# One matmul for folded squares, a first gate pair in the common order, and a smaller first transfer

## The chip, the cores and the metric

The kernel runs on one core of one Trainium2 chip. The metric is the device time of one execution in microseconds (us). Engines are named as in the profile: PE is the matrix engine (PEld its weight loads), DVE the vector engine, ACT the scalar engine, POOL the general-purpose engine, SP the one that issues most transfers. A name with q (SPq, ACTq) is an engine's issue of a transfer.

## The reference

One layer over 512 tokens of width 2048, in float32. Three token mixers run side by side on projections of the same normalised input; C is stick-breaking attention, B chunked attention with a relative bias, A attention with forget gates. Each has four heads of width 128.

```python
hn = rmsnorm(x, norm_g)
proj = jnp.einsum('bsd,dc->bsc', hn, w_in)
br = proj[..., :QKVG_COLS].reshape(b, s, N_BRANCH, 4, BRANCH_W)   # q, k, v, g of A, B, C
gates = jax.nn.sigmoid(proj[..., QKVG_COLS + N_HEADS:] + b_gate).reshape(b, s, N_BRANCH, D_MODEL)
qa = rmsnorm(to_heads(br[:, :, 0, 0]), qk_norm_g[0])              # likewise ka, qb, kb; not in C
...
ys = jnp.stack([from_heads(ya), from_heads(yb), from_heads(yc)], axis=2) * jax.nn.silu(br[:, :, :, 3])
up = jnp.einsum('bsnw,nwd->bsnd', ys, w_up)
merged = jnp.sum(gates * up, axis=2)
return x + jnp.einsum('bsd,de->bse', merged, w_out)
```

## The kernel before

Everything is held transposed: a tile has 128 features on the partitions and the 512 tokens along the row. To keep float32 accuracy each operand is split into a high part in the matrix engine's reduced format and a low part, the rest (`split`: ACT copies the high part, DVE subtracts for the low one). A product is then high x high, high x low and low x high.

The projections come as pairs of 128-column blocks (`PairTask`). A pair is computed by Strassen's scheme on the two halves of the tokens (256 each) and the two halves of the 2048 inputs, with seven products, numbered 1 to 7. Each product is a unit (`Pair`) of eight steps over the inputs. In the usual form a step of the high weight part reads both parts of x at once as one matmul of 512 columns, and a step of the low weight part reads the high x as one of 256. Products that are added up share an accumulator bank: 6 goes onto 1, 7 onto 6, 4 onto 7, 3 onto 5 (`onto`), after ACT has copied what was there. The order of these products is 1, 2, 6, 5, 7, 3, 4.

The first gate pair, which follows the first four projections, has a form of its own, chosen by `late=True`: the order 1, 5, 2, 3, 6, 7, 4, each step of the high weight part as two matmuls of 256 columns, and no sharing of banks, so that sums are done by DVE from separate banks.

A weight for a product is loaded by SP as a raw tile. Two of the five raw tiles of a pair get a second block added in the transfer (`add_up`, issued by POOL); two more sums are made by DVE (`sums`): block 1 plus block 5 is the weight of product 6, and that plus block 2 the weight of product 3. `prep` splits a weight two units ahead of its use.

The first unit group (`first_quad`) computes Q, K, V and G of head C0 as x arrives; x is also scaled by the norm's gain (`prep_x`), squared for its norm, and its Strassen combinations (t23, t4) are made in `combos`. The forget gates' logits come from small matmuls against w2 (`logits`). Sixteen matmuls on constants (WARM) run on PE before any data is there.

Q and K of the eight heads of B and A are normalised in `normed`: square the tile, split the square, multiply both parts by a matrix of ones to sum over the 128 partitions, take the reciprocal root, scale, and split again (qkh, qkl). Scores read these parts.

The order of PE, ACT and DVE is fixed in the program. A planner (`Flow`) sets it: each task yields its steps with an engine and an estimated cost, and the planner repeatedly takes the step that can start first, ties by due time. `at(u, ...)` starts a side task when unit u begins. Buffers (`Slots`) are counted there as well, so a step's place also depends on when buffers come free. What the planner doesn't order (transfers) is issued in the order in which the tasks ask.

Of the kernel before, what the change touches and what calls it, by code (L numbers as in the profile page):

```python
# [8 lines left out]
F32 = mybir.dt.float32  # L9
F32R = mybir.dt.float32r  # L10
BF16 = mybir.dt.bfloat16
AF = mybir.ActivationFunctionType
ALU = mybir.AluOpType
AX = mybir.AxisListType

P = 128
S = 512
D = 2048
HD = 128
NH = 4  # L20
W = 512
NB = 3
KT = D // P
QB = S // P
DT = D // P
UK = 8
NQ = 4
HS = S // 2
EPS = 1e-6
NEG = -1e30  # L30
SCALE = HD ** -0.5
# [4 lines left out]
PE, ACT, DVE = 0, 1, 2  # L36
# [26 lines left out]
class Flow:  # L63
# [98 lines left out]
def hybrid_kernel(  # L162
# [2 lines left out]
    xT: bass.AP,  # L165
    xn: bass.AP,
    begin: bass.AP,
    w_one: bass.AP,
    w_two: bass.AP,
    w_col: bass.AP,  # L170
# [5 lines left out]
    nc = tc.nc  # L176
    PS = bass.MemoryType.PSUM

    cp = ctx.enter_context(tc.tile_pool(name="cp", bufs=1))
# [35 lines left out]
    def blk(i):  # L215
        return slice(i * P, (i + 1) * P)
# [22 lines left out]
    def pair_of(name, dt=F32R):  # L239
        return t2(name + "h", dt), t2(name + "l", dt)  # L240

    def split(hi, lo, src, n, ev=None, due=(), hi_ev=None):

        yield (ACT, act_us(n), *due)
        nc.scalar.activation(hi, src, AF.Copy)  # L245
        if hi_ev is not None:
            set_(hi_ev)
        yield (DVE, dve_us(n), *due)
        nc.vector.tensor_sub(lo, src, f(hi))  # L249
        if ev is not None:  # L250
            set_(ev)
# [38 lines left out]

    nc.scalar.preload_act_table_set("natural_log_exp_and_others")
    begin_in = cp.tile([P, begin.shape[1]], F32, name="begin_in")
    x_begin, small_in = begin_in[:, :S], begin_in[:, S:]
    first = [tc.keep_in_program_order(nc.sync.dma_start(begin_in, begin))]
    gn = small_in[:, 0:KT]
    gqk = small_in[:, KT:KT + 4]
    bfc = small_in[:, KT + 4:KT + 5]
    bg = small_in[:, KT + 5:KT + 5 + NB * DT]
    wf = small_in[:, KT + 5 + NB * DT:].rearrange("p (k h) -> p k h", h=NH)

    epsc = cp.tile([P, 1], F32, name="epsc")
    nc.gpsimd.memset(epsc, EPS)
    nhepsc = cp.tile([P, 1], F32, name="nhepsc")
    nc.gpsimd.memset(nhepsc, -0.5 * EPS)
    tmpc = t2("tmpc")
    onef, zerof, nu_f = tmpc[:, blk(0)], tmpc[:, blk(1)], tmpc[:, blk(2)]
    nc.gpsimd.memset(onef, 1.0)
    nc.gpsimd.memset(zerof, 0.0)
    ones_r = cp.tile([P, P], F32R, name="ones_r")
    nc.vector.tensor_copy(ones_r, onef)  # L310
# [14 lines left out]
    nc.gpsimd.memset(zeroc, 0.0)  # L325

    gq = cp.tile([P, 4], F32, name="gq")
    nc.vector.tensor_copy(gq, gqk)
    for c in (0, 2):
        nc.vector.tensor_scalar_mul(gq[:, c:c + 1], gqk[:, c:c + 1], SCALE)  # L330

    w2 = cp.tile([P, KT * NH + 32], F32, name="w2")
    nc.vector.tensor_copy(w2[:, :KT * NH].rearrange("p (k h) -> p k h", k=KT), wf)
    nc.vector.tensor_copy(w2[:, KT * NH:], zerof[:, :32])
    t2s.free.pop()


# [88 lines left out]
    def prep_x(kt):  # L426

        due = (2.5 + 2.7 * place[kt],)
        yield x_in[kt]
        x, g, h, lo = xraw[kt], gn[:, kt:kt + 1], xs[kt].hi, xs[kt].lo  # L430
        if kt == 0:
            yield (DVE, 0.5, *due)
            nc.vector.tensor_scalar_mul(h, two(x), g)
        else:
            yield (ACT, act_us(S), *due)
            nc.scalar.activation(h, two(x), AF.Copy, scale=g)
        set_(raw_hi[kt])
        yield (DVE, dve_us(S), *due)
        nc.vector.scalar_tensor_tensor(lo, two(x), g, f(h), op0=ALU.mult, op1=ALU.subtract)
        set_(raw_ev[kt])  # L440

        due = (DUE[0] - 16.0 + place[kt],)
        if kt % 2 == 0:
            yield (DVE, 0.5, *due)
            nc.vector.tensor_scalar_mul(x, x, g)
# [435 lines left out]
    class Head:  # L881
# [23 lines left out]
        def normed(self, r):  # L905
            yield self.event(r)
            c = self.c[r]
            yield from by_norm(c)
            yield t2s, 3
            yield ACT, act_us(S)  # L910
            sq = t2("sq")
            nc.scalar.activation(sq, c, AF.Square)
            hi, lo = pair_of("sq")
            yield from split(hi, lo, sq, S)
            give(t2s)
            yield atts, 1
            yield PE, mm_us(S, 2)
            ps = att()
            nc.tensor.matmul(ps, ones_r, hi, start=True, stop=False)  # L919
            nc.tensor.matmul(ps, ones_r, lo, start=False, stop=True)  # L920
            give(t2s, 2)
            yield t2s, 4
            rs = t2("rs")
            yield from rsqrt(rs, ps, HD, (t2("rt"), t2("rw"), t2("rv")), S, lambda: give(atts))
            give(t2s, 3)
            i = 2 * self.n + r
            yield DVE, dve_us(S)
            nc.vector.scalar_tensor_tensor(rs, rs, gq[:, i:i + 1], c, op0=ALU.mult, op1=ALU.mult)
            give(t2s)
            yield t2s, 2  # L930
            self.c[r] = pair_of("qk")
            yield from split(*self.c[r], rs, S, self.event("p", r))
            give(t2s)
# [338 lines left out]
    def first_head(n, h):  # L1272
        hd = Head(n, h)
        units.extend(first_quad(hd))
        at(OFF["fb"], forget_bias)
        gate_units(late=True)
        schedule(hd, OFF["a0"], OFF["b0"])

    def head(n, h, last=False):
# [220 lines left out]
    def loads():  # L1500
        def x(kt):
            if kt == 0:
                xraw[kt], x_in[kt].t = x_begin, landing(0.0, 256)
                return
            yield t2s, 1
            xraw[kt] = t2("x")
            x_in[kt].t = fetch(xraw[kt], xT[kt], 0.0, 256).t

        def n(i):
            yield t2s, 1  # L1510
            t = t2("xn")
            n_in[i].t = fetch(t, xn[i // NQ, i % NQ], 0.0, 256).t
            spawn(square_x(i, t), 10.0)

        todo = list(range(NQ * QB))
        for i, sp in enumerate(spans):

            for kt in [kt for sp in spans[i:i + (2 if i > 2 else 1)] for kt in range(*sp)]:
                if xraw[kt] is None:
                    yield from x(kt)  # L1520
            yield from load_unit(units[i])
            if i >= N_FROM:
                for _ in range(N_PER):
                    if todo:
                        yield from n(todo.pop(0))
        for i in todo:
            yield from n(i)
        for u in units[len(spans):]:
            yield from load_unit(u)
# [27 lines left out]
    spawn(loads(), 0.0, 0.0)  # L1557
    for kt in range(KT):
        spawn(prep_x(kt), 5.0)
    for k in range(UK):  # L1560
        spawn(combos(k), 5.0)
    spawn(stream(), 1e9)
# [4 lines left out]
NT = 20  # L1567
KEPT = 1
AHEAD = 0.4
WARM = 16  # L1570
SPANS = [(0, 1), (1, 2)] + [(k + h, k + h + 2) for k in range(0, UK, 2) for h in (0, UK)][1:]
N_ONE = 2
NX = 28
# [56 lines left out]
```

## Time and profile before

| | |
|---|---|
| median of 3 runs | 1318.89 us (1318.42 to 1319.12) |
| profiled execution | 1318.54 us, span 1316.8 us |
| granted PE clock | 1.000 |
| PE busy | 1311.3 us (100%), 7474 matmuls |
| DVE / ACT / POOL busy | 1140.6 / 807.2 / 95.0 us |
| bytes moved | 266.24 MB, 202 GB/s |

The span is the time from the first to the last instruction in the profile; what lies around it makes up the difference to the execution's time. In rows of the timeline the columns are start, duration, engine, line, operation, what is written from what, shapes, and how many instructions were merged into the row; a bracket gives the idle time before it and what ended it. A row with several instructions has as its duration the time from the first start to the last end, and ends of matmuls are modelled, so a matmul's price is read from one start to the next.

### The profile page before, as it was taken

How to read it: one execution, taken by the hardware profiler on the slowest of the kernel's cores; microseconds unless marked ns; L12 is line 12 of the kernel's file. 1: busy time of each engine (PE TensorE's matmuls, PEld its weight loads, DVE VectorE, ACT ScalarE, POOL GpSimd, SP SyncE). 2: the span in 40 equal slices, each digit the busy share in tenths (PEclk: the TensorE clock that was granted, in tenths of full speed). 3: DMA queues.
4: the chain of work that ended last, by engine and by line, in shares of the span. 5: the costliest groups of instructions: out<-in, count | busy, mean ns of one | idle time of the engine just before them, and what ended most of it. 6: DMA issues, size and time to landing. Idle time of an engine off the chain costs nothing.

```text
span 1316.8 us, 20264 instructions
## 1 busy us (share of the span) xinstructions
PE 1311.3 (100%) x7474; PEld 1149.1 (87%) x7474; DVE 1140.6 (87%) x1707; ACT 807.2 (61%) x1280; POOL 95.0 (7%) x120
## 2 busy tenths in 40 slices
PE   9999999999999999999999999999999999999998
PEld 6898888888888888888888888888888888898887
DVE  8999989788898889888898989889899988897786
ACT  8766757575557665666656664666657655454443
POOL 0010100000010100101000000001000000000100
PEclk9999999999999999999999999999999999999999
DMA  9777767767776776766767767776769765668883
GB/s 339 213 204 198 183 192 185 200 186 192 201 199 187 188 200 179 219 181 189 202 179 216 188 184 199 205 185 185 195 179 280 248 219 168 206 172 253 242 248 100
DMA packets 89651, 266.24 MB, mean 202 GB/s; under 512 B 10560, under 2 KB 12608, under 8 KB 89552
## 3 DMA queue, kind: packets, MB, share of 16 engines
q1 hardware_dynamic: 70400, 203.86, 45.5%
q0 software_dynamic: 15552, 56.63, 25.4%
q10 hardware_dynamic: 3600, 4.46, 0.9%
q8 instruction: 59, 0.97, 0.3%
q14 instruction: 40, 0.33, 0.1%
HBM read 245.21 MB, written 19.70 MB: 201 GB/s over the span
## 4 chain that ended last, share of the span: by engine, by line
PE 99%; DVE 1%; DMA 0%; ACT 0%; issue 0%; ACTq 0%
PE acc L264 85%; PE att L264 8%; PE att L1022 1%; PE att L260 1%; PE att L1136 1%; PE att L261 1%; PE att L1137 1%; PE att L259 1%; PE att L1135 1%; PE att L1087 0%; PE att L1237 0%; PE att L919 0%; PE att L920 0%; DMA begin_in<-in_begin 0%; DVE m L249 0%; DVE wl L249 0%
## 5 line engine op out<-in xcount | busy, mean ns | idle before, releaser
L249 DVE TENSOR_TENSOR wl<-raw,wh 128x1024 fp32r<-128x1024 f32 (+2 forms) x418 | 499.0, 1198 | 122.2 <-ACT wh L245 121.5
L245 ACT ACTIVATE wh<-raw 128x1024 fp32r<-128x1024 f32 (+2 forms) x418 | 433.7, 1039 | 162.9 <-PE acc L264 89.9
L264 PE MATMUL acc<-x,wh 128*128 128x512 f32 (+1 forms) x1568 | 396.7, 388 | 0.7 <-DVE gq L330 0.7
L264 PEld LDWEIGHTS acc<-x,wh 128*128 128x128 f32 x1568 | 283.7, 188 | 56.1 <-issue 2.2
L264 PE MATMUL acc<-t,wh 128*128 128x512 f32 (+1 forms) x1128 | 280.3, 388 | 0.0
L264 PEld LDWEIGHTS acc<-t,wh 128*128 128x128 f32 x1128 | 200.4, 189 | 34.8
L264 PEld LDWEIGHTS acc<-x,wl 128*128 128x128 f32 x1504 | 205.9, 190 | 16.5 <-issue 0.8
L264 PE MATMUL acc<-x,wl 128*128 128x256 f32 (+1 forms) x1504 | 216.5, 285 | 0.0
L264 PE MATMUL acc<-t,wl 128*128 128x256 f32 x1104 | 156.5, 283 | 0.0
L264 PEld LDWEIGHTS acc<-t,wl 128*128 128x128 f32 x1104 | 144.7, 191 | 2.1
L282 POOL DMA_DIRECT2D raw<-in_w_col x92 | 79.7, 866 | 916.3 <-DMA raw<-in_w_col 449.3
L264 PE MATMUL acc<-m,wh 128*128 128x512 f32 (+1 forms) x512 | 109.7, 364 | 0.3 <-DVE m L249 0.3
L264 PEld LDWEIGHTS acc<-m,wh 128*128 128x128 f32 x512 | 86.3, 189 | 13.9 <-DVE m L249 0.5
L825 ACT ACTIVATE c<-acc 128x256 f32<-128x256 f32 x51 | 19.6, 384 | 90.8 <-PE acc L264 85.3
L771 ACT ACTIVATE u<-acc 128x512 f32<-128x512 f32 x52 | 31.1, 598 | 65.6 <-PE acc L264 60.3
L631 DVE TENSOR_TENSOR raw<-raw,raw 128x1024 f32<-128x1024 f32 x54 | 65.8, 1219 | 0.3
L637 DVE TENSOR_TENSOR raw<-raw,raw 128x1024 f32<-128x1024 f32 x54 | 65.8, 1218 | 0.3
L264 PE MATMUL att<-y,wh 128*128 128x512 f32 x256 | 65.8, 389 | 0.0
L792 ACT ACTIVATE u<-acc 128x512 f32<-128x512 f32 x51 | 30.3, 595 | 55.1 <-PE acc L264 54.2
L264 PEld LDWEIGHTS acc<-m,wl 128*128 128x128 f32 x448 | 58.3, 191 | 2.4
L264 PE MATMUL acc<-m,wl 128*128 128x256 f32 x448 | 59.8, 283 | 0.0
L264 PEld LDWEIGHTS att<-y,wh 128*128 128x128 f32 x256 | 48.0, 188 | 10.0
(202 smaller groups left out, 1388.6 us busy)
## 6 DMA issues: line engine op xcount, KB each, us to landing
raw<-in_w_col SPq DMA_DIRECT2D x230, 512.0 KB, 4.4
raw<-in_w_col POOLq DMA_DIRECT2D x92, 512.0 KB, 6.4
raw<-in_w_out SPq DMA_DIRECT2D x40, 512.0 KB, 4.3
gl<-c SPq DMA_DIRECT2D x48, 256.0 KB, 3.1
raw<-in_w_up SPq DMA_DIRECT2D x32, 384.0 KB, 3.1
sg<-gl SPq DMA_DIRECT2D x48, 256.0 KB, 4.4
raw<-in_w_out POOLq DMA_DIRECT2D x16, 512.0 KB, 7.3
xn<-in_xn SPq DMA_DIRECT2D x16, 256.0 KB, 3.6
```

Source lines behind the costliest of these rows:

```text
L245: nc.scalar.activation(hi, src, AF.Copy)
L249: nc.vector.tensor_sub(lo, src, f(hi))
L259: nc.tensor.matmul(ps, lh, rh, start=start, stop=False, skip_group_check=more)
L260: nc.tensor.matmul(ps, lh, rl, start=False, stop=False, skip_group_check=more)
L261: nc.tensor.matmul(ps, ll, rh, start=False, stop=stop, skip_group_check=more)
L264: nc.tensor.matmul(ps, w, x, start=start, stop=stop, skip_group_check=more)
L282: nc.gpsimd.dma_start(to, src, accum_op=ALU.add)
L631: nc.vector.tensor_add(w[1], w[1], w[5])
L637: nc.vector.tensor_add(w[2], w[2], w[1])
L771: nc.scalar.activation(self.u, ps, AF.Copy)
L792: nc.scalar.activation(self.s, ps, AF.Copy)
L825: nc.scalar.activation(c, ps[:, RH], AF.Copy, scale=-1.0)
```

## The change

Four things change.

1. `normed`: the lower and the upper 64 partitions of the tile are squared into two tiles of 64 partitions, and DVE adds them. The sum is split with its high part in partitions 0 to 63 and its low part in 64 to 127 of one tile, so that one matmul with the ones sums both.
2. The first gate pair loses `late=True`: product order 1, 2, 6, 5, 7, 3, 4, sums in the banks, 512-column matmuls in the high parts.
3. The first transfer (begin) holds only x's first tile and the norm gains, 528 columns instead of 645. The other constants (117 columns) are a transfer of their own, issued by ACT after its weight load. What reads them on DVE (gq, w2) becomes a planned task, `small_parts`.
4. The constant ones are written first on POOL, and WARM goes from 16 to 19.

```diff
-    x_begin, small_in = begin_in[:, :S], begin_in[:, S:]
+    small_in = cp.tile([P, consts.shape[1]], F32, name="small_in")
+    x_begin, gn = begin_in[:, :S], begin_in[:, S:]
...
+    def small_parts():
+        yield DVE, 0.8
+        nc.vector.tensor_copy(w2[:, :KT * NH].rearrange("p (k h) -> p k h", k=KT), wf)
+        nc.vector.tensor_copy(gq, gqk)
+        for c in (0, 2):
+            nc.vector.tensor_scalar_mul(gq[:, c:c + 1], gqk[:, c:c + 1], SCALE)
...
-            yield ACT, act_us(S)
-            sq = t2("sq")
-            nc.scalar.activation(sq, c, AF.Square)
-            hi, lo = pair_of("sq")
-            yield from split(hi, lo, sq, S)
+            yield ACT, act_us(S, 2)
+            sa, sb = t2("sa"), t2("sb")
+            nc.scalar.activation(sa[:HP], c[:HP], AF.Square)
+            nc.scalar.activation(sb[:HP], c[HP:], AF.Square)
+            yield DVE, dve_us(S)
+            nc.vector.tensor_add(sa[:HP], sa[:HP], sb[:HP])
+            give(t2s)
+            parts = t2("sq", F32R)
+            yield from split(parts[:HP], parts[HP:], sa[:HP], S)
             give(t2s)
             yield atts, 1
-            yield PE, mm_us(S, 2)
+            yield PE, mm_us(S)
             ps = att()
-            nc.tensor.matmul(ps, ones_r, hi, start=True, stop=False)
-            nc.tensor.matmul(ps, ones_r, lo, start=False, stop=True)
-            give(t2s, 2)
+            nc.tensor.matmul(ps, ones_r, parts, start=True, stop=True)
+            give(t2s)
...
-        gate_units(late=True)
+        gate_units()
...
+            if i == 0:
+                nc.scalar.dma_start(small_in, consts)
...
+    spawn(small_parts(), 2.0, 9.0)
...
-WARM = 16
+WARM = 19
```

The order of instructions moves at three places. DVE at the first data, before (x_113 is the high part of x's first tile and then its low part, wl_194 or wl_195 the low part of the first weight):

```order
L334 COPY w_108<-tmpc_85 128x32
L328 COPY gq<-begin_in 128x4
L333 COPY w_108<-begin_in 128x64
L433 TENSOR_SCALAR x_2_113<-begin_in 128x2x256
L330 TENSOR_SCALAR gq<-begin_in 128x1 x2
L439 TENSOR_SCALAR x_2_113<-begin_in,x_2_113 128x2x256
L445 TENSOR_SCALAR begin_in<-begin_in 128x512
L392 TENSOR_TENSOR wl_195<-raw_150,wh_194 128x512
```

and in the change:

```order
L331 COPY w_106<-tmpc_82 128x32
L438 TENSOR_SCALAR x_2_110<-begin_in 128x2x256
L444 TENSOR_SCALAR x_2_110<-begin_in,x_2_110 128x2x256
L450 TENSOR_SCALAR begin_in<-begin_in 128x512
L397 TENSOR_TENSOR wl_196<-raw_150,wh_195 128x512
```

The copies and products for gq and w2 are gone from in front of x's parts; they come back between the parts of x's third and fourth tiles.

DVE where the first gate pair is fed, before (wl_623 is the low weight part of product 5, wl_557 of 1, raw_512 plus raw_509 the weight of product 6, c_686 and c_688 are copies of the first four projections):

```order
L249 TENSOR_TENSOR wl_623<-raw_509,wh_622 128x1024
L249 TENSOR_TENSOR wl_557<-raw_512,wh_556 128x1024
L249 TENSOR_TENSOR t_92_541<-x_174,t_92_541 128x256
L1223 COPY c_686<-acc_204 128x512
L1223 COPY c_688<-att_206 128x512
L631 TENSOR_TENSOR raw_512<-raw_512,raw_509 128x1024
```

and in the change (wl_562 is the low part of product 1, wl_628 of 2, wl_695 of 6; L636 and L642 are the two sums of raw weights):

```order
L251 TENSOR_TENSOR wl_562<-raw_517,wh_561 128x1024
L251 TENSOR_TENSOR t_92_546<-x_175,t_92_546 128x256
L636 TENSOR_TENSOR raw_517<-raw_517,raw_514 128x1024
L1231 COPY c_691<-acc_205 128x512
L1231 COPY c_693<-att_207 128x512
L251 TENSOR_TENSOR wl_628<-raw_519,wh_627 128x1024
L251 TENSOR_TENSOR t_103_650<-x_181,t_103_650 128x256
L251 TENSOR_TENSOR t_101_635<-x_191,t_101_635 128x256
L251 TENSOR_TENSOR t_102_647<-x_193,t_102_647 128x256
L642 TENSOR_TENSOR raw_519<-raw_519,raw_517 128x1024
L251 TENSOR_TENSOR wl_695<-raw_517,wh_694 128x1024
```

The low part of 5 has left the front of this stretch, and the first sum has moved ahead of the two copies.

DVE at the first normalised head, K and Q of B0, before (sql are the low parts of the squares, the wl rows those of weights):

```order
L249 TENSOR_TENSOR sql_3835<-sq_3832,sqh_3834 128x512
L249 TENSOR_TENSOR wl_3851<-raw_3687,wh_3850 128x1024
L249 TENSOR_TENSOR sql_3847<-sq_3844,sqh_3846 128x512
L249 TENSOR_TENSOR wl_3887<-raw_3651,wh_3886 128x1024
L249 TENSOR_TENSOR wl_3923<-raw_3710,wh_3922 128x1024
```

and in the change (sa is a folded square of 64 partitions, sq the tile with both parts):

```order
L920 TENSOR_TENSOR sa_3799<-sa_3799,sb_3800 64x512
L251 TENSOR_TENSOR wl_3795<-raw_3635,wh_3794 128x1024
L251 TENSOR_TENSOR sq_3816<-sa_3780,sq_3816 64x512
L251 TENSOR_TENSOR sq_3820<-sa_3799,sq_3820 64x512
L251 TENSOR_TENSOR wl_3826<-raw_3599,wh_3825 128x1024
```

The two additions (the row ahead of this piece is the other) stand before the same weight part, and both low parts of the squares follow it.

More of the change, by code (lines that the diff above doesn't have):

```diff
@@ L16 @@
 P = 128
+HP = P // 2
 S = 512
@@ L167, in hybrid_kernel @@
     begin: bass.AP,
+    consts: bass.AP,
     w_one: bass.AP,
@@ L292, in hybrid_kernel @@
     begin_in = cp.tile([P, begin.shape[1]], F32, name="begin_in")
-    x_begin, small_in = begin_in[:, :S], begin_in[:, S:]
+    small_in = cp.tile([P, consts.shape[1]], F32, name="small_in")
+    x_begin, gn = begin_in[:, :S], begin_in[:, S:]
     first = [tc.keep_in_program_order(nc.sync.dma_start(begin_in, begin))]
[L295 to L299, printed above, removed]
+    gqk = small_in[:, 0:4]
+    bfc = small_in[:, 4:5]
+    bg = small_in[:, 5:5 + NB * DT]
+    wf = small_in[:, 5 + NB * DT:].rearrange("p (k h) -> p k h", h=NH)
+    tmpc = t2("tmpc")
+    onef, zerof, nu_f = tmpc[:, blk(0)], tmpc[:, blk(1)], tmpc[:, blk(2)]
+    nc.gpsimd.memset(onef, 1.0)
     epsc = cp.tile([P, 1], F32, name="epsc")
@@ L304, in hybrid_kernel @@
     nc.gpsimd.memset(nhepsc, -0.5 * EPS)
-    tmpc = t2("tmpc")
-    onef, zerof, nu_f = tmpc[:, blk(0)], tmpc[:, blk(1)], tmpc[:, blk(2)]
-    nc.gpsimd.memset(onef, 1.0)
     nc.gpsimd.memset(zerof, 0.0)
@@ L327, in hybrid_kernel @@
     gq = cp.tile([P, 4], F32, name="gq")
-    nc.vector.tensor_copy(gq, gqk)
-    for c in (0, 2):
-        nc.vector.tensor_scalar_mul(gq[:, c:c + 1], gqk[:, c:c + 1], SCALE)
     w2 = cp.tile([P, KT * NH + 32], F32, name="w2")
-    nc.vector.tensor_copy(w2[:, :KT * NH].rearrange("p (k h) -> p k h", k=KT), wf)
     nc.vector.tensor_copy(w2[:, KT * NH:], zerof[:, :32])
+    def small_parts():
[4 more added lines that the diff above has]
+            nc.vector.tensor_scalar_mul(gq[:, c:c + 1], gqk[:, c:c + 1], SCALE)
     t2s.free.pop()
@@ L1610 @@
         "xn": g["x"][0].reshape(QB, P, DT // NQ, S).transpose(0, 2, 1, 3),
-        "begin": np.concatenate([xT[0]] + consts, axis=1),
+        "begin": np.concatenate([xT[0], consts[0]], axis=1),
+        "consts": np.concatenate(consts[1:], axis=1),
         "w_one": np.stack([first(*sp) for sp in SPANS[:N_ONE]]),
```

## The prediction

> **What bounds the kernel now.** I read the page first, its busy times and its chain.
>
> ```profile
> span 1316.8 us, 20264 instructions
> PE 1311.3 (100%) x7474; PEld 1149.1 (87%) x7474; DVE 1140.6 (87%) x1707; ACT 807.2 (61%) x1280; POOL 95.0 (7%) x120
> PE 99%; DVE 1%; DMA 0%; ACT 0%; issue 0%; ACTq 0%
> ```
>
> PE is occupied for all but 5.5 us of the span and carries 99% of the chain that ended last. Ends of matmuls are modelled, so a wait could hide under that share. The waits of PE, which are read from starts, answer this:
>
> ```profile
> PE att L1553 <- POOL tmpc L307: 1.1, 1, 1.1
> PE acc L264 <- DVE gq L330: 0.7, 1, 0.7
> PE acc L264 <- DVE m L249: 0.3, 1, 0.3
> ```
>
> These are three waits in the whole program, two of them before the first real product. So time is what PE executes, plus the beginning and the end; a matmul taken out shortens the span by its start-to-start time, as long as nothing PE reads comes later than now. The windows show how much slack the others have in the stages that the change touches:
>
> ```profile
> core 0: us, PE busy (x) PEld busy (x) DVE busy (x) ACT busy (x) POOL busy (x), PEclk, DMA share, GB/s
> 4.00:4.50 0.50, 0.50 (x4) 0.18 (x2) 0.00 (x0) 0.00 (x0) 0.00 (x0) 1.00 1.05 406
> 6.00:30.00 24.00, 24.00 (x116) 16.94 (x115) 23.76 (x41) 23.53 (x44) 0.00 (x0) 1.00 1.04 387
> 54.80:75.80 21.00, 21.00 (x176) 20.90 (x175) 20.71 (x32) 12.84 (x25) 1.72 (x2) 1.00 0.68 182
> 700.00:1000.00 300.00, 300.00 (x1744) 265.39 (x1743) 269.93 (x409) 187.95 (x294) 25.08 (x29) 1.00 0.72 194
> ```
>
> DVE is the neighbour to watch: 23.8 of 24 us at the beginning, 20.7 of 21 in the first gate pair, 90% in the heads.
>
> **Folded squares, one matmul (16 times: Q and K of the eight A and B heads).** In the timeline, the first of them before:
>
> ```profile
> 354.69 1.14 ACT L912 ACTIVATE sq<-c 128x512 f32<-128x512 f32 x2
> 358.42 0.39 PE L919 MATMUL att<-sqh,ones_r 128*128 128x512 f32 x1
> 358.66 0.39 PE L920 MATMUL att<-sql,ones_r 128*128 128x512 f32 x1
> 358.85 0.68 DVE L249 TENSOR_TENSOR sql<-sq,sqh 128x512 fp32r<-128x512 f32 x1
> 358.89 0.40 PE L264 MATMUL acc<-t,wh 128*128 128x512 f32 x1
> 365.18 1.98 PE L264 MATMUL acc<-x,wh 128*128 128x512 f32 x8
> 366.99 1.11 PE L264 MATMUL acc<-x,wl 128*128 128x256 f32 x8
> 367.95 1.12 PE L264 MATMUL acc<-t,wl 128*128 128x256 f32 x8
> ```
>
> From start to start the second matmul costs 358.89 - 358.66 = 0.23 us; eight of the same width take 366.99 - 365.18 = 1.81, or 0.226 each. One goes at each place: 16 x 0.23 = **3.7 us**, between 3.6 and 3.8. In return each place gets one more square on ACT (half of 1.14, 0.57: an estimate, since 64 partitions with 512 elements each have no row here; a row per partition count would lie between 0 and that) and one DVE addition (0.68). Neither stands on the path as long as PE has other products to run: the chain from a column to its normalised parts grows by about 1.2 us, and what reads it are the scores, some 30 us later. What is near there:
>
> ```profile
> 389.89 0.68 DVE L249 TENSOR_TENSOR qkl<-rs,qkh 128x512 fp32r<-128x512 f32 x1
> 391.42 0.19 PEld L260 LDWEIGHTS att<-qkl,qkh 128*128 128x128 f32 x1
> ```
>
> The last part is there at 390.57 and PE loads it at 391.42, so the cover is only 0.85 us. I still cost the longer chain at nothing, for two reasons. In the changed order the second qkl still stands between the same sum of raw weights and the same low weight part on DVE, and the scores stand at the same product of the stream; and the matmul's own operands now hold one buffer where they held two, so the buffers for which this chain queues come free no later. If that fails, it is the second rival.
>
> **The first gate pair.** Its form before, and that of every other pair (365.18 to 367.95, above):
>
> ```profile
> 57.65 2.08 PE L264 MATMUL acc<-x,wh 128*128 128x256 f32 x16
> 59.57 1.12 PE L264 MATMUL acc<-x,wl 128*128 128x256 f32 x8
> 60.53 2.08 PE L264 MATMUL acc<-x,wh 128*128 128x256 f32 x16
> ```
>
> A product takes 60.53 - 57.65 = 2.88 us with sixteen 256-column matmuls for the high part, and 367.95 - 365.18 = 2.77 with eight of 512. Seven products: 7 x 0.11 = 0.77; starts are read to a hundredth, which makes 0.1 over seven, so I take **0.7 us**, bounds 0 and 0.8. The row makes two 256-column matmuls cost 2 x 0.12 = 0.24 against 0.226. The Trainium skill, page "TensorE: Matmul & The Clock Gate", section "Back-to-back issue gap", gives an isolated gap of N/2.4 + 2.5 ns, so that splitting a matmul costs 2.5 ns; by it the pair would save an estimated 56 x 2.5 ns = 0.14 us. The trace disagrees with that (0.12 us for 256 columns where the page has 0.109); the page's case is close to the third rival.
>
> I go by the rows.
>
> The order becomes 1, 2, 6, 5, 7, 3, 4, so product 6 is third instead of fifth and needs its summed weight earlier. The feed before:
>
> ```profile
> raw<-in_w_col POOLq DMA_DIRECT2D x1, 512.0 KB, 9.1
> 43.12 1.01 POOL L282 DMA_DIRECT2D raw<-in_w_col  x1 [40.89 <-DVE small_n L488]
> 52.26 2.01 ACT L245 ACTIVATE wh<-raw 128x1024 fp32r<-128x1024 f32 x2 [1.26 <-DMA raw<-in_w_col]
> 54.78 2.08 PE L264 MATMUL acc<-x,wh 128*128 128x256 f32 x16
> 57.16 1.21 DVE L631 TENSOR_TENSOR raw<-raw,raw 128x1024 f32<-128x1024 f32 x1
> 66.44 2.08 PE L264 MATMUL acc<-t,wh 128*128 128x256 f32 x16
> ```
>
> The adding transfer, issued at 43.1, lands 9.1 us later at 52.2, and the high part of product 5 waited for it. In the changed order product 1 is split first and needn't wait: its high part can be made at 51.0 to 52.1, its low part by 53.3, and the sum (L631 before, L636 now) follows at 53.7 to 54.9 in place of 57.2. After it DVE has two copies that wait for the quad's end at 54.8 (0.6 each), the low part of 2 (1.2), three small splits (0.35 each), the other sum (1.2) and then the low part of 6: about 60.8. PE starts product 6 at 54.5 + 2 x 2.77 = 60.0 with the high part and wants the low one at 61.8. The same count gives 64.8 for product 7, whose low part comes first, wanted at 65.4. So margins are 1.0 and 0.6 us where 6 started at 66.4 before: no wait, but little to spare. The copies out of the banks that 6, 7 and 4 add onto have over 1 us each. The sums done in the bank take a few DVE instructions away there; DVE is not the bound, so this counts for nothing.
>
> **The beginning.** The warm-up, the chain from begin to the first matmul, the rows of the other operand, and three later ones:
>
> ```profile
> 1.13 3.48 PE L1553 MATMUL att<-tmpc 128*128 128x256 bf16 x16 [1.13 <-POOL tmpc L307]
> 4.50 0.17 DVE gq L328
> 4.67 0.10 DVE w L333
> 4.77 0.40 DVE x L433
> 5.31 0.70 PE acc L264 x2
> 4.69 0.72 ACT L388 ACTIVATE wh<-raw 128x256 fp32r<-128x256 f32 x2 [2.61 <-DMA raw<-in_w_one]
> 5.28 0.30 PEld L264 LDWEIGHTS acc<-x,wh 128*128 128x128 f32 x2 [1.04 <-ACT wh L388]
> 7.13 0.30 PEld L264 LDWEIGHTS acc<-x,wl 128*128 128x128 f32 x2 [0.16 <-DVE wl L392]
> 10.10 1.22 DVE L249 TENSOR_TENSOR wl<-raw,wh 128x1024 fp32r<-128x1024 f32 x1
> 15.60 0.73 PE L264 MATMUL acc<-x,wl 128*128 128x512 f32 x2
> ```
>
> Two operands meet at 5.3. For x, two small DVE instructions (4.77 - 4.50 = 0.27) go from in front of it, and the transfer shrinks by 58.5 KB of 322.5 KB (117 of 645 columns), at the 406 GB/s of the window about 0.15 us. For the weight only the second helps, since it shares the DMA engines. So the first matmul comes between 0.03 (5.31 - 5.28, weight unmoved) and 0.42 us earlier; the weight decides, and I take 0.2. The wait of about 0.1 at 7.13 also goes, because the low weight part no longer queues behind the gq instructions. Together **0.3 us**, from 0 to 0.5. What is moved: consts is one more transfer issued on ACT's queue ahead of its split, in ACT's idle 2.61 us: nothing. It takes one of the eight completion slots that the loads share, so four x loads on SP wait for one landing more and are issued somewhat later; the DMA engines are full then (1.05), so bytes flow as before: nothing. The four DVE instructions (the two of 0.27 and two more products, 0.6 at most) now stand just ahead of an x split and of the low weight part that is made from 10.1 to 11.3 and read at 15.6: covered by over 4 us. Three more warm-up matmuls at the 0.22 us of before (sixteen in 3.48) end by 5.2 at the latest, and PE had nothing else: 0 to 0.1.
>
> **Sum.** 3.7 + 0.7 + 0.3 = 4.7 us. The profiled execution took 1318.54 us (span 1316.8 plus 1.7 around it): 1313.8. It lies 0.35 below the median of the runs shown, 1318.89, and the forecast is for the median: **1314.2 us**, -0.36%. About 0.2%, or 2.6 us, is what a measurement of this kernel can tell from no change.
>
> **Rivals.**
> (1) *The gate pair waits.* Should the adding transfer or the DVE queue run 2 us later than counted, PE waits 1 to 1.4 us at product 6 or 7 and keeps it: about 1315.5; a 3 us delay gives 1316.5. For it: DVE at 20.7 of 21 us and margins of 0.6 and 1.0. Against: the rows moved forward start on things that were there at 52.2. 8%.
> (2) *The scores wait, and it gets slower.* The normalised parts have 0.85 us of cover at each of eight heads, and all that stands behind the scores on PE would wait with them. If the 1.2 us more were not absorbed and also pushed qkl behind one more low weight part (1.2), PE would wait 2.4 - 0.85 = 1.55 us eight times: 12.4 - 4.7 = 7.7 us more, 1326.6. It decides from 0.92 us per head on, that is qkl 1.8 us later than now. Half of that delay would give no change, about 1317. Against: the qkl rows keep their places in DVE's order, and buffers, not arithmetic, fill most of those 30 us. 4% for slower, 4% for nothing left.
> (3) *Splitting columns costs nothing.* If two matmuls of 256 columns took what one of 512 takes, the pair would save nothing and the sum be 4.0: 1314.9. The 0.12 us rows speak against it. 5%.
> (4) *PE's work is not the time.* If waits are hidden under modelled ends, DVE at 90% in the heads would set the pace and its extra 16 x 0.6 us would use up the gain: about 1318.5. Starts that repeat to the hundredth (57.65, 59.57 and 60.53 lie 16 and 8 times 0.12 apart) speak against it. 2%.
>
> **Chances and range.** The forecast has 77%. With (3) and (1), 90% is faster by over 0.2%; 6% within 0.2% ((4) and half of (2)); 4% slower. The low end takes the best of every term (3.8 + 0.8 + 0.6) and the 0.3 us by which single runs differ: 1313.3. The high end reaches into the first rival, 1316.0. Outside lie parts of (1), (2) and (4).
>
> **What the profile after would show.** 16 fewer ones_r matmuls and none of 256 columns in the high parts of the gate pair; the first product at about 5.0 to 5.1 us; the quad's end some 0.3 us earlier than 54.78; a gate pair of 2.77 us per product; PE's waits still under 1 us from there on; a span of about 1312.1. A PE wait on DVE at a low weight part near 62 to 65 us would be the first rival, a wait on qkl at the first scores of a head the second. If the span shrinks by less than 2.6 us with no new wait listed for PE, start-to-start times are not what a matmul is worth, and the whole reading is wrong.

## The result, and the profile after

The changed kernel takes 1313.42 us (median of 6, 1313.13 to 1313.56) where the kernel before took 1318.96 in the same comparison (median of 6, 1318.41 to 1320.61): a ratio of 0.9957, 95% interval 0.9947 to 0.9968. That is faster, by 5.5 us where 4.7 were forecast. Put against the median that was known it is 1318.89 x 0.9957 = 1313.2, 0.1 us below the range. The interval of the ratio is wider than that (1311.9 to 1314.7), so the times alone do not say which term of the sum was too small; the parts, read from traces below, do. The profiled execution took 1313.15 us. The page of after, span, busy times and chain:

```profile
span 1311.4 us, 20146 instructions
PE 1306.7 (100%) x7405; PEld 1143.5 (87%) x7405; DVE 1154.3 (88%) x1723; ACT 817.8 (62%) x1298; POOL 94.8 (7%) x120
PE 99%; DVE 0%; ACT 0%; issue 0%; POOL 0%; ACTq 0%; POOLq 0%
```

PE still fills the span, with 69 matmuls fewer; DVE is busy for 13.7 us more and ACT for 10.6, and neither shows in the chain. The waits of PE, all that are listed (the list leaves out the shortest gaps):

```profile
PE att L1563 <- POOL nhepsc L309: 1.1, 1, 1.1
PE acc L266 <- DVE m L251: 0.3, 1, 0.3
```

The wait of 0.7 us for gq is gone and none has come. The timeline of PE at the first data and in the first gate pair, after:

```profile
3.17 1.79 PE L1563 MATMUL att<-tmpc 128*128 128x256 bf16 x9
4.92 0.72 PE L266 MATMUL acc<-x,wh 128*128 128x512 f32 x2
...
54.43 1.98 PE L266 MATMUL acc<-x,wh 128*128 128x512 f32 x8
56.24 1.11 PE L266 MATMUL acc<-x,wl 128*128 128x256 f32 x8
57.20 2.00 PE L266 MATMUL acc<-x,wh 128*128 128x512 f32 x8
59.04 1.12 PE L266 MATMUL acc<-x,wl 128*128 128x256 f32 x8
59.99 2.00 PE L266 MATMUL acc<-t,wh 128*128 128x512 f32 x8
```

The first product starts at 4.92 (5.31 before), the quad (the first four projections) ends at 54.43 (54.78), and a product of the gate pair takes 2.77 to 2.79 us (2.88). Product 6 starts at 59.99 without a gap. From there on PE has one listed wait, the 0.3 us for m, and it is the same before and after. So the rest can be read between two fixed points: the first gate product (the quad's end) and the start of the very last matmul. Before it is 1258.34 us, after 1253.35. The experiments are read by this stretch, because what comes ahead of it changes from run to run by more than the effects in question.

The times of the kernel before fall into two groups: of its 77 executions in all comparisons 48 took 1318.4 to 1319.4 us (median 1318.89) and 29 took 1320.2 to 1321.1. Its profile, and the three times that I had, are of the lower group; the changed kernel shows one group. The last experiments are about this.

### The profile page after: what moved, and what is told of

Read it like the earlier page. It is cut to its first block, busy times and chain, and to the rows that moved or that the text cites. A ratio compares the mean times of both kernels' runs of the same rounds, so it can differ in the third digit from the quotient of the medians.

```text
span 1311.4 us, 20146 instructions
## 1 busy us (share of the span) xinstructions
PE 1306.7 (100%) x7405; PEld 1143.5 (87%) x7405; DVE 1154.3 (88%) x1723; ACT 817.8 (62%) x1298; POOL 94.8 (7%) x120
## 4 chain that ended last, share of the span: by engine, by line
PE 99%; DVE 0%; ACT 0%; issue 0%; POOL 0%; ACTq 0%; POOLq 0%
PE acc L266 85%; PE att L266 8%; PE att L1030 1%; PE att L262 1%; PE att L1144 1%; PE att L263 1%; PE att L1145 1%; PE att L261 1%; PE att L1143 1%; PE att L1095 0%; PE att L1245 0%; PE att L1563 0%; PE att L928 0%; DVE m L251 0%; ACT wh L247 0%; DVE wl L251 0%
## 5 line engine op out<-in xcount | busy, mean ns | idle before, releaser
L266 PE MATMUL acc<-x,wh 128*128 128x512 f32 x1536 | 394.1, 392 | 0.0
L266 PE MATMUL acc<-t,wh 128*128 128x512 f32 x1104 | 278.9, 393 | 0.0
L642 DVE TENSOR_TENSOR raw<-raw,raw 128x1024 f32<-128x1024 f32 x54 | 65.9, 1221 | 0.5
L636 DVE TENSOR_TENSOR raw<-raw,raw 128x1024 f32<-128x1024 f32 x54 | 65.9, 1220 | 0.3
```

Source lines behind the costliest of these rows:

```text
L266: nc.tensor.matmul(ps, w, x, start=start, stop=stop, skip_group_check=more)
L636: nc.vector.tensor_add(w[1], w[1], w[5])
L642: nc.vector.tensor_add(w[2], w[2], w[1])
```

## Experiments: each part alone

**Squares alone.** The kernel before with `normed` as in the change and nothing else; of its edit the matmul:

```diff
-            nc.tensor.matmul(ps, ones_r, hi, start=True, stop=False)
-            nc.tensor.matmul(ps, ones_r, lo, start=False, stop=True)
+            nc.tensor.matmul(ps, ones_r, parts, start=True, stop=True)
```

> The kernel before with the folded squares alone (16 ones_r matmuls where there were 32). Flat theory, the prediction's: a matmul is worth its 0.23 us wherever it stands, so 16 x 0.23 = 3.7 us: span 1316.8 - 3.7 = 1313.1, and the step from one A or B head to the next falls from 84.37 to 83.91 us. Place theory: before, the two matmuls stood among matmuls of 512 columns, and after each interruption the next four of these run at 236, 228 to 229, 232 and 231 ns instead of 227, so that a head's four cost 0.97; now its two stand among matmuls of 256 columns and cost 0.44. Then 8 x 0.53 = 4.24: span 1312.6, step 83.84 us. Third: the rest of the gain comes only from all parts together; then this kernel shows 3.7 or less.

Measured: from the quad's end to the last matmul 1254.00 us; a step from head to head 83.84 us (the 384-column scores of two heads lie at 393.50 and 561.18, two heads apart). The place theory's 83.84 is met to the hundredth, the flat theory's 83.91 is not. The span, 1314.6, is no test here, since its first product came at 5.82 us and its first microseconds ran slowly (see below). Time: 1316.47, ratio 0.9972 (0.9962 to 0.9982); six of its eight runs, the profiled one among them, are of its upper group (1316.0 to 1317.1), and the other two took 1314.91 and 1315.09.

**Gate pair alone.** The kernel before with one line changed:

```diff
-        gate_units(late=True)
+        gate_units()
```

> The kernel before with the first gate pair in the order and form of the others, nothing else. As predicted: 0.7 us (bounds 0 to 0.8), span 1316.1. By the two traces: the pair from first product to the next pair takes 20.22 us where it took 20.99, 0.77 less, of which about 0.16 is a short gap that the old pair had at 63.6 us (two starts of 56 and 103 ns over the usual ones); span 1316.0. If splitting of columns cost nothing the pair would give only the 0.16.

Measured: 1257.54 us from the quad's end to the last matmul, 0.80 less than before. Not all of it is the pair's form: two other traces with the old form show 1258.20 (19 and 28 warm-ups, below), because the short gap at 63.5 is not in them. PE's timeline before, and then with 19 warm-ups:

```profile
62.45 1.12 PE L264 MATMUL acc<-x,wl 128*128 128x256 f32 x8
63.47 2.17 PE L264 MATMUL acc<-x,wh 128*128 128x256 f32 x16
65.48 0.76 PE L264 MATMUL acc<-x,wl 128*128 128x256 f32 x5
```

```profile
62.56 1.12 PE L264 MATMUL acc<-x,wl 128*128 128x256 f32 x8
63.52 2.08 PE L264 MATMUL acc<-x,wh 128*128 128x256 f32 x16
65.44 0.76 PE L264 MATMUL acc<-x,wl 128*128 128x256 f32 x5
```

From 62.45 to 65.48 are 3.03 us, from 62.56 to 65.44 2.88. So the form is worth 1258.20 - 1257.54 = 0.66 us, and 0.14 is a gap of the old form. It goes with how late the weight of product 5, which comes by the adding transfer, is split before the quad's end: ACT begins at 52.26 before, 2.5 us ahead of 54.78, and 3.1 and 3.5 us ahead in the two traces without the gap. The ratio, 0.9992 (0.9983 to 1.0001), can't tell this from nothing, but the groups can: 8 of its 11 runs took 1317.89 to 1318.34, less than any run of before, and 3 are of an upper group.

**Beginning alone.** The kernel before with the smaller begin, `consts`, `small_parts`, POOL's order and 19 warm-ups.

> The kernel before with the new beginning alone (528 instead of 645 columns, constants on ACT's queue, small DVE work moved, POOL's ones first, 19 warm-ups). As predicted: 0.3 us (0 to 0.5). By the two traces: the first product starts at 4.92 instead of 5.31 and the quad ends at 54.43 instead of 54.78: 0.35 us, span 1316.45, and from there on every start is earlier by that same 0.35. If the gain at the beginning is lost later in waits, the later starts show less.

The expectation failed: from the quad's end to the last matmul it takes 1258.82 us, 0.62 more than 1258.20, and the quad doesn't end sooner either. The rows of PE with a wait in its gate pair, and ACT's splits of the pair's first two weights, product 5's and behind it product 1's:

```profile
55.19 2.18 PE L266 MATMUL acc<-x,wh 128*128 128x256 f32 x16 [0.23 <-ACT wh L247]
64.35 1.81 PE L266 MATMUL acc<-x,wh 128*128 128x256 f32 x13 [0.26 <-ACT wh L247]
```

```profile
53.13 2.01 ACT L247 ACTIVATE wh<-raw 128x1024 fp32r<-128x1024 f32 x2 [1.94 <-DMA raw<-in_w_col]
```

The first product starts at 5.26 in this trace (5.31 before), and the quad's last matmul at 54.58, so that without the wait the quad would end at 54.81, as before. But product 5's weight, which comes by the adding transfer, is split from 53.13 on, where that was 52.26 before: it landed later, product 1's split stood behind it, and PE waited ahead of the pair's first product and once more at 64.35. The changed kernel splits product 1's weight at 50.64 and shows no such wait. That the beginning's gain would be lost without the new order of the pair is not shown by this: in this one trace there was no gain to lose, and it is of the longest of the 11 runs (1319.43). The times (1318.73, ratio 0.9991, 0.9983 to 1.0000, all runs between 1318.07 and 1319.43) show mostly the missing second group; their median lies 0.16 us below that of before's lower group.

The parts of squares and gate pair add up: 1258.20 - 0.66 - 4.20 = 1253.34, and after has 1253.35.

## Experiments: what a matmul costs in its place

In PE's timeline before, the first norm place, and an ordinary stretch of the same shape (sixteen 512-column matmuls, sixteen of 256):

```profile
356.80 1.78 PE L264 MATMUL acc<-t,wh 128*128 128x512 f32 x7
...
359.12 1.32 PE L264 MATMUL acc<-x,wh 128*128 128x512 f32 x5
360.28 0.39 PE L919 MATMUL att<-sqh,ones_r 128*128 128x512 f32 x1
360.51 0.39 PE L920 MATMUL att<-sql,ones_r 128*128 128x512 f32 x1
360.74 0.86 PE L264 MATMUL acc<-x,wh 128*128 128x512 f32 x3
361.44 1.11 PE L264 MATMUL acc<-x,wl 128*128 128x256 f32 x8
362.38 1.12 PE L264 MATMUL acc<-t,wl 128*128 128x256 f32 x8
363.34 0.86 PE L264 MATMUL acc<-t,wh 128*128 128x512 f32 x3
...
342.87 2.00 PE L264 MATMUL acc<-t,wh 128*128 128x512 f32 x8
344.71 1.98 PE L264 MATMUL acc<-x,wh 128*128 128x512 f32 x8
346.53 1.12 PE L264 MATMUL acc<-x,wl 128*128 128x256 f32 x8
347.48 1.12 PE L264 MATMUL acc<-t,wl 128*128 128x256 f32 x8
348.44 0.86 PE L264 MATMUL acc<-t,wh 128*128 128x512 f32 x3
```

The ordinary stretch takes 348.44 - 342.87 = 5.57 us, the one with four ones_r matmuls (ones_r is the matrix of ones) 363.34 - 356.80 = 6.54: they cost 0.97, or 0.243 each. After, the two of them stand in the low part:

```profile
355.64 2.00 PE L266 MATMUL acc<-t,wh 128*128 128x512 f32 x8
357.48 1.98 PE L266 MATMUL acc<-x,wh 128*128 128x512 f32 x8
359.30 0.51 PE L266 MATMUL acc<-x,wl 128*128 128x256 f32 x3
359.65 0.40 PE L928 MATMUL att<-sq,ones_r 128*128 128x512 f32 x1
...
360.35 0.39 PE L928 MATMUL att<-sq,ones_r 128*128 128x512 f32 x1
...
361.65 2.00 PE L266 MATMUL acc<-t,wh 128*128 128x512 f32 x8
```

361.65 - 355.64 = 6.01, so 0.44 for two. The rows of the ordinary stretch show the reason: eight 512-column matmuls take 344.71 - 342.87 = 1.84 after a low part and 346.53 - 344.71 = 1.82 after a high one. In the trace's single starts they go at 233, 236, 228, 233, 231 and then 227 ns, and an interruption by another product begins that anew (236, 229, 232, 231, 227 after the first two ones_r matmuls before). The 256-column matmuls that follow an interruption mostly take 117 to 119 ns instead of 120. The longer chain of the folded squares reaches PE later, and the planner put them among these.

Two kernels move only the place. The first is the changed kernel with the ones_r matmuls planned later, into the high parts:

```diff
+            yield Event(flow.fin + (3.0 if r == Q else 2.5))
             yield atts, 1
```

> The changed kernel, in which the planner places the 16 ones_r matmuls some 3 us (Q) and 2.5 us (K) later, so that all stand between matmuls of 512 columns, where they stand between matmuls of 256. Same instructions, same count. Flat theory: no change, span 1311.4, step from head to head 83.84 us. Place theory: a single interruption costs 0.26 there against 0.22, so 16 x 0.04 = 0.66 us more: span 1312.1, step 83.92 us. If the later place makes scores wait, PE shows waits on qk parts, and it gets slower by more than that.

Measured: 1253.71 us, 0.36 more than after; 1313.95 us in all. It goes the way of the place theory with about half of its amount: the same stretch takes 6.07 us where it took 6.01. The first of the two matmuls came after the first four of a run, and the second four later, when the starts of the others were still slow (235, 229, 232 and 233 ns between the two), so that less was left to spoil.

The second is the kernel before with its 32 matmuls planned 1.5 and 3 us later, into the low parts, by the same line.

> The kernel before, in which the planner places the 32 ones_r matmuls 1.5 us (Q) and 3 us (K) later, so that all stand among matmuls of 256 columns where they stand among 512. Same instructions, same count. Read from the end of the first quad to the last matmul, 1258.34 us before. Flat theory: 1258.3. Place theory: a head's four matmuls cost 0.44 + 2 x 0.23 = 0.90 there instead of 0.97, so 8 x 0.07 = 0.6 us less: 1257.8, and the step between heads 84.30 instead of 84.37.

Measured: 1257.65 us, 0.55 less than 1258.20, with not one instruction fewer; the step between heads 84.30. That is as expected. Seven of its ten runs took 1317.99 to 1318.42 (median 1318.21, 0.68 below that of before's lower group), three are of an upper group. So of the 4.20 us of the squares 0.55 is place and 3.65 the sixteen matmuls, 0.228 each.

**Splitting columns.** The dispute between rows and rule, on a large dose:

```diff
-                            yield PE, mm_us(S)
-                            mm(two(self.ps[p]), u.hi[:, j, :], r, start, stop, more)
+                            for i in range(2):
+                                yield PE, mm_us(HS)
+                                mm(two(self.ps[p])[:, i, :], u.hi[:, j, :], r[:, i, :], start and i == 0, stop, more or i == 1)
```

> The changed kernel with every 512-column matmul of the high weight parts of all pairs made as two of 256 columns: 2960 matmuls more, each with a weight load of its own. By the rows (2 x 0.120 against 0.2266 inside a run, and two products in 5.76 against 5.57 us with the changes between runs): 370 products x 0.095 = 35.2 us more, span about 1346.6. By the page's isolated gap of N/2.4 + 2.5 ns a split costs 2.5 ns: 7.4 us more, 1318.8. If DVE at 88% sets part of the pace, less than 35.2, since DVE's work stays the same.

Measured: 10365 matmuls, 1287.26 us, 33.91 more than after, 1347.91 us in all, ratio 1.0215 (1.0201 to 1.0229). That is 11.5 ns for each split. The rows' 35.2 is near; 7.4, from the isolated gap in the Trainium skill ("TensorE: Matmul & The Clock Gate", "Back-to-back issue gap"), is not what this stream does.

## Experiments: the first microseconds

**19 warm-ups in the kernel before.**

> The kernel before with 19 warm-up matmuls instead of 16, nothing else. In the runs of the four kernels so far, those with 16 fall into two groups (before: 1318.7 to 1319.1 and 1320.3 to 1321.0) and those with 19 into one; in two traces of the slow group PE stood still for 1.3 and 1.5 us between the last warm-up and the first product, and the first eight or nine matmuls then took 427 ns from start to start instead of 227. Theory of the gap: three more warm-ups shorten it below 0.8 us (no slow matmul in the trace with 0.8), so all runs are at 1318.4 to 1319.2. Rival: the slow group comes from a late landing of the first data itself, by 0.5 us and more; then two groups remain, 1 to 2 us apart.

Of 11 runs 9 took 1318.48 to 1319.4 and 2 took 1320.82 and 1320.99 (median 1318.98, ratio 0.9999, 0.9990 to 1.0008). The upper group is still there (whether it is rarer than 29 of 77, 11 runs can't tell), so the theory of the gap in that form is wrong. The trace of the kernel before with the ones_r matmuls planned into the low parts says so as well. PE's timeline of squares alone, and then of that one, both with 16 warm-ups:

```profile
3.02 1.70 PE L1557 MATMUL att<-tmpc 128*128 128x256 bf16 x7
5.82 1.19 PE L265 MATMUL acc<-x,wh 128*128 128x512 f32 x2 [1.10 <-DVE gq L331]
6.82 1.05 PE L265 MATMUL att<-x,wh 128*128 128x512 f32 x2
7.67 0.63 PE L265 MATMUL acc<-x,wh 128*128 128x512 f32 x1
```

```profile
3.03 1.35 PE L1554 MATMUL att<-tmpc 128*128 128x256 bf16 x7
5.66 0.70 PE L264 MATMUL acc<-x,wh 128*128 128x512 f32 x2 [1.28 <-DVE gq L330]
6.20 0.61 PE L264 MATMUL att<-x,wh 128*128 128x512 f32 x2
6.65 0.62 PE L264 MATMUL acc<-x,wh 128*128 128x512 f32 x2
```

Both waited more than a microsecond. In the second the seven last warm-ups took 1.35 us, so PE had gone to full rate while they ran, and two products start 0.45 us apart (6.65 - 6.20); in the first the warm-ups stayed slow to the end, and two products take 0.85 (7.67 - 6.82), until 9.2 us. What counts is whether the higher rate is granted before the first product. It needn't come while the warm-ups run: in the changed kernel with 16 of them (below) these were 0.21 us apart to the end, and the products ran at full rate from the first, at 5.33 us, on. The Trainium skill has the rule ("TensorE: Matmul & The Clock Gate", "What's actually happening"): half rate until PE has been busy through a window of 3413 ns, and the windows run freely, with no regard to the kernel's start. These traces agree: the rate went up at about 4.0 us in one run and 9.2 in the other, with the same kernel start.

How much of a window must be busy is my estimate, made with the 3413 ns of the Trainium skill as its length. PE works from 1.13 us on, so the 3.4 us ahead of 4.0 hold 2.8 us of work, and these were enough. The window ahead of 9.2 begins at 5.8, and the one before it, from 2.4 on, holds 2.3 us of work up to the end of the warm-ups at 4.72; these were not. The bounds of a window themselves show in no trace.

**Warm-ups of the changed kernel at 10 and at 16, and 28 in the kernel before.** One number changes in each.

> The changed kernel with 10 warm-up matmuls instead of 19, nothing else. They end at about 3.3 us and the first product can start at 4.9 to 5.4, after 1.6 us and more. Theory of the gap: the first matmuls run at 427 ns for some 3.4 us, eight at 0.2 us more: 1.6 us, so 1315.0 in every run. Rival (warm-ups only fill time, the rate of the products does not depend on them): 1313.4 as with 19.

Measured: 1315.73 us (1314.85 to 1316.26), all seven runs at least 1.4 us above 1313.42; the median is 0.7 above the expected 1315.0. Its timeline and a window of it:

```profile
5.32 1.22 PE L266 MATMUL acc<-x,wh 128*128 128x512 f32 x2 [1.94 <-ACT wh L393]
6.34 1.05 PE L266 MATMUL att<-x,wh 128*128 128x512 f32 x2
7.19 1.05 PE L266 MATMUL acc<-x,wh 128*128 128x512 f32 x2
8.04 0.77 PE L266 MATMUL att<-x,wh 128*128 128x512 f32 x2
8.65 0.62 PE L266 MATMUL acc<-x,wl 128*128 128x512 f32 x2
9.11 0.62 PE L266 MATMUL att<-x,wl 128*128 128x512 f32 x2
```

```profile
5.40:8.00 2.60, 2.60 (x6) 2.07 (x7) 2.56 (x5) 2.42 (x5) 0.00 (x0) 1.00 1.04 404
```

Pairs 0.85 us apart become pairs 0.46 apart after 8.4 us, while the granted clock of the window ahead of that reads 1.00; this halving has to be looked for in the starts. The stretch from the quad's end on is 1253.34, as after: all of the loss lies ahead of it.

> The changed kernel with 16 warm-up matmuls instead of 19, nothing else. Theory of the window: PE's rate is raised only after a stretch of some 3.4 us that is busy nearly all through (2.8 of 3.4 us were enough in one trace, 2.3 were not in another), at instants that shift from run to run; 16 warm-ups end at about 4.5 us, the data come at 4.9 to 5.4, and in part of the runs the stretch has too much idle time in it. Then a slow group 1 to 2 us above 1313.4 appears, as in before, though in fewer runs, since the data come 0.4 us earlier. Rival (late landing of the data made the slow group of before, and the new beginning ended that): one group at 1313.1 to 1313.6.

Measured: four runs at 1313.52 to 1313.69 and one at 1315.95. The theory of the window has it so, but it is one run of five, and there is no trace of it.

> The kernel before with 28 warm-up matmuls instead of 16, nothing else: they end between 5.9 and 6.7 us, so PE doesn't stand still before the data even where these land late. Theory of the window: no run in the group of 1320.3 to 1321.1; all within about 1318.5 to 1319.6, since up to 0.6 us may be lost to warm-ups that are still running when early data are there. Rival (late landing itself makes the slow group): runs above 1320.3 remain in a third or so of the executions.

Measured: 1318.65 to 1319.99 in 11 runs, median 1318.91 (ratio 0.9999, 0.9990 to 1.0008): no run of the upper group, though its data come no sooner (DVE's first copy from begin starts at 4.77 us in its trace, at 4.50 before). One run, at 1319.99, is longer than the 1319.6 that I expected at most. So late data alone don't make that group, and it goes when PE has no idle time ahead of the data; that this works by the windows is the reading that fits, not one that a trace shows. The median stays (1318.92 for the kernel before in that set, with 4 of 15 runs in the upper group), since most runs were in the lower one.

## Experiment: a further step

The changed kernel with a rule for the planner: matmul groups of squares, scores and attention products wait (six places in all) until no high part is running and until, by the planner's count, their operands are there. The line stands at each of the six places:

```diff
+            yield lambda: not high_now[0] and flow.ready + MARGIN <= flow.clock[PE]
             yield PE, mm_us(S)
```

> The changed kernel with one rule more for the planner: the small matmul groups that sums of squares, scores and attention products put between the pairs' products may not stand inside a run of 512-column matmuls; they wait for the next low part. In the order 40 groups leave such runs: 44 stand where a high part ends and its low part begins, 21 inside low parts. Same instructions. Place theory: an interruption of a 512-column run costs 0.034 us more than one of a 256-column run (the 16 places of the two-matmul squares gained 0.55 us by moving), so 40 x 0.034 = 1.4 us less: 1252.0 us from the quad's end to the last matmul in place of 1253.35, and about 1312.0 us in all. Flat theory: 1253.35, no change. Rival: the later scores (by up to 3.7 us) reach what reads them too late, PE shows waits, and it gets slower.

> The changed kernel itself, beside the one with the rule for the planner, for a comparison on the same chip: 1313.1 to 1313.6 us, 1253.35 us from the quad's end to the last matmul, and no run 1.5 us above the others.

Measured: 1313.14 us (1313.01 to 1313.19), ratio 0.9949 (0.9935 to 0.9962), against 1313.83 (1313.52 to 1314.16) and 0.9954 (0.9942 to 0.9967) for the changed kernel itself. The two sets of times don't overlap, though the intervals of the ratios do. From the quad's end it takes 1252.86, 0.49 less than 1253.35. The changed kernel missed its own expectation here: its trace of this set had 1253.93, with 0.58 us in short gaps between 1012 and 1018 us that its first trace doesn't have, so not all of the 0.69 us between the two medians need be the rule's. No new wait is listed after the first product. It has the lowest median of all that ran, by the stretch with a third of the gain that I expected. A likely reason, not tested, is that the price of 0.034 us, taken from 512-column sums, is too high for groups that are mostly score and transpose matmuls of 128 to 512 columns.

## Why the prediction was right in kind and short in size

The account of the profiled runs, 1316.83 - 1311.41 = 5.42 us. The terms for squares and gate pair come from traces of their own, the last two from the one pair of traces:

| step | predicted | measured | from |
|---|---|---|---|
| squares, 16 matmuls | 3.7 (3.6 to 3.8) | 4.20 | squares alone against 1258.20 |
| ... of it the place | not seen | 0.55 | matmuls of before planned lower |
| gate pair | 0.7 (0 to 0.8) | 0.66, and 0.14 for a gap | gate pair alone |
| beginning | 0.3 (0 to 0.5) | 0.35 | quad's end, 54.78 and 54.43 |
| after the last matmul | 0 | 0.07 | 3.70 and 3.63 us |

- **PE as the bound, no new waits:** right. 99% of the chain before and after, and both lists of waits show it; the lists leave out short gaps, though, and one of 0.14 us was hidden there.
- **Squares:** the step that failed is the price, 16 x 0.23. I read one matmul's start-to-start time and gave it bounds of 3.6 to 3.8, as if its neighbours didn't change. The order of the changed kernel was at hand and showed the matmuls among 256-column ones; I used it for the scores and not for this. The sixteen matmuls alone were worth 3.65, and their place 0.55 more. 0.5 of the missing 0.72 us lies here.
- **The cover of the scores,** 0.85 us: right. After, the last part ends at 388.88 and is loaded at 389.73, again 0.85 us; rival (2) did not come. The timeline of DVE and PE's weight loads:

```profile
388.20 0.68 DVE L251 TENSOR_TENSOR qkl<-rs,qkh 128x512 fp32r<-128x512 f32 x1
389.73 0.19 PEld L262 LDWEIGHTS att<-qkl,qkh 128*128 128x128 f32 x1
```

- **Gate pair:** the size was right (0.66 for 0.7). Rival (1) did not come: the low part for product 6 was there at 60.06, wanted at 61.83. What I had missed is the short gap of the old form; the list of waits doesn't have it, but the starts do. A slip on the way: product 7 was due at 54.5 + 4 x 2.77 = 65.6, not 65.4.
- **Rival (3), splitting free:** fell by 33.91 us against 7.4.
- **Beginning:** 0.35, within its bounds, but partly luck. One reading was wrong: the 0.16 us at 7.13, which I counted as 0.1, is a wait of the weight load alone, and PE's starts there are the usual 0.23 us apart. So nothing was to be gained after the first product, and from there to the quad's end it takes 49.47 us before and 49.51 after; the first product itself came 0.39 earlier. And the size is that of one pair of traces: the changed kernel beside the planner's rule ends its quad at 54.78, with 16 warm-ups at 54.87, and the kernel before with 19 warm-ups at 54.89. The medians, 1318.89 of the lower group and 1313.42, are 5.47 apart; without the 4.86 of squares and gate pair some 0.6 are left for the beginning, the gap and the end, so a gain is there, but its size is known to a few tenths only.
- **Warm-ups:** I priced three more at 0 to 0.1. In the kernel before they left the median as it was and 2 of 11 runs in the upper group. In the changed kernel none of 11 runs with 19 is in an upper group, and one of five with 16; more runs would have to show that this is their doing. The upper group costs 1.9 us in about four of ten runs of the kernel before, which the one profile that I had, of the lower group, could not show.
- **After the last matmul:** 0.07 us, priced at nothing. The traces with the new beginning have 3.62 to 3.64 us there and those with the old one 3.70 to 3.72; why is open.
- **Range:** its low end took 3.8 for the squares; with 4.2 it would have held the time. (1318.89 - 5.2 - 0.3 is 1313.4, where I wrote 1313.3.)

## What to carry to other kernels

Where PE is the bound, price a removed matmul by a whole stretch with and without it, not by its own start-to-start time, and look in the new order at what its neighbours will be. A gain at one place lasts only if what the next stage reads is there sooner too: in the beginning alone, PE waited for a weight that landed late. Before trusting one profile for an effect at the start, look at the spread of many runs: two groups of times mean something that one trace can't show.

## What the hardware showed

- After a run of 256-column matmuls, those of 512 columns start 233, 236, 228, 233 and 231 ns apart before they settle at 227; after an interruption by another product it is 236, 229, 232 and 231. Inside a run 256 columns settle at 120 ns and 384 mostly at 175; these three fit columns/2.4 plus 13.4 ns within 2 ns. 128 columns do not: most of them are 108 to 110 ns apart.
- When PE has stood still, even for 56 ns, the next start comes 0.10 us late as well: in a 256-column run it follows after 223 ns instead of 120, before (63.47 us), in the beginning alone (64.35) and in the second trace of the changed kernel (1012.12).
- PE's first microseconds can run at half rate, in one trace until 9.2 us from the span's start, with a granted clock of 1.00 in the windows (read in the kernel with 10 warm-ups, 5.40 to 8.00 us).
- These instructions cost no less on 64 partitions than on 128: ACT's squares of 64x512 take 0.63 us each, where two of 128x512 took 1.14 before, and DVE's addition of 64x512 takes 0.68 like the subtraction on 128x512 before. The timeline of ACT after:

```profile
353.53 0.62 ACT L917 ACTIVATE sa<-c 64x512 f32<-64x512 f32 x1
354.16 0.63 ACT L918 ACTIVATE sb<-c 64x512 f32<-64x512 f32 x1
```
